# One core, a DiT layer in f32: the last four down-projection blocks multiplied by the gate ahead of their split, tile 1's residual summed in PSUM, and tile 1's other columns closed by one operation and a rank-one product

## The chip, the cores and the metric

The kernel runs on one NeuronCore of one Trainium2 chip. The metric is the device time of one execution in microseconds (us). Of the kernel before there are three timed runs, and one further execution that the hardware profiler recorded; the rows below are from that one.

The engines are named as the profile names them: PE (TensorE: matmuls, with PEld for its weight loads), DVE (VectorE), ACT (ScalarE), POOL (GpSimd) and SP (SyncE, which here only issues DMAs). PSUM is the memory in which PE leaves its products; a bank of it holds 128x512 f32.

## The reference, cut to what matters

One layer of a diffusion transformer, 256 latent tokens and 256 context tokens of width 2048, all f32. The change touches the end of it alone: the second half of the feed-forward part, its gated residual and the last layer norm.

```python
DN_ALPHA = (2.0 * DEPTH) ** 0.25        # DEPTH = 1

def layer_norm(x, g, b):
    mu = jnp.mean(x, axis=-1, keepdims=True)
    var = jnp.mean(jnp.square(x - mu), axis=-1, keepdims=True)
    return (x - mu) * lax.rsqrt(var + EPS) * g + b

def swiglu(u, w_gate, w_up, w_down):
    return (jax.nn.silu(u @ w_gate) * (u @ w_up)) @ w_down

...
x = layer_norm(DN_ALPHA * x + g1 * (heads @ w_out), ln1_g, ln1_b)
x = layer_norm(DN_ALPHA * x + g2 * swiglu(modulate(x, sh2, sc2), w_gate, w_up, w_down), ln2_g, ln2_b)
```

`w_down` is 5632 x 2048. `g2` is one vector of 2048, the same for all tokens.

## The kernel before

The 256 tokens are two tiles of 128 rows (`NT = 2`, t = 0 and 1), one token to a partition. The 2048 output columns are four chunks of `NB = 512` (n = 0 to 3). The 5632 hidden units are eleven groups f of 512, each of four pieces j of 128. `hTh[f]` and `hTl[f]` hold the hidden values transposed, as a high and a low part.

**Split products.** PE multiplies in the fast f32r form, so every f32 operand is split: ACT casts it to a high part (L230), DVE subtracts to get the low part (L231). `mm3` (L239 to L242) makes one product of three matmuls: high by high (L240), high by low weight (L241), low by high weight (L242). `load_split` loads a weight block of 512 hidden units by 512 columns (1 MB, SP queue, `raw`) and splits it in two halves of 128x1024, in tiles `hi` and `lo`; `RAW_BUFS = 4` raw tiles and `HL_BUFS = 4` of each half are there. A block gives 4 pieces x 2 tiles x 3 = 24 matmuls of 128x512.

**The end of the program.** `pair(n)` does two chunks, n and n + 1. Its list `two[0]` does chunk 2 (for some groups f by a scheme of quarters, `by_quarters`), its list `two[1]` chunk 3, in the banks "b" (tile 0) and "d" (tile 1); `whole`, returned as `two[6]`, is the order of the groups f that are not done by quarters. `plain` does one block: split, then tile 0's twelve matmuls, then tile 1's. `combine_parts`, `first_block` and `gated` multiply a finished bank by the gate (`g2[i]`, each two chunks wide) and add it to the residual base `xt`, which already holds ALPHA times the first layer norm's output.

The last four blocks of chunk 3 are handled apart: they are split into rooms that are free by then (`wide`, in the place of a tile that is no longer used, the usual `hi` and `lo`, and `hilo`, in the place of a raw tile), so that all four are there at once, and PE does tile 0 through all four and then tile 1 through all four.

**The ending.** `gated(t, 3, ...)` multiplies the bank by the gate (L1153) and adds it to `xt` (L1154), `spread` takes the statistics of chunk 3 (L1157; those of the other chunks are there already), `ln_scalars(t, True)` gets mean and 1/sqrt(var + EPS) by three Newton steps, the first on DVE (L1176, L1177), the other two on ACT (L1172 to L1174), `first_step` (L1674, four times) does (x - mean) * ln2_g, `last_step` (L1678, four times) does x * y + ln2_b, y being the root, and stores the chunk.

**What sets the order.** The program is written as one stream; a scheduler orders each engine's instructions, by its own estimate of the times, except for engines named in a `manual_schedule`, which keep the order of the text. The order is fixed in the built program. Before, the last four blocks' loads and splits are ordered by the scheduler, and only the ending itself is in the order of the text on DVE and ACT.

## Time and profile before

| | us |
|---|---|
| timed runs | 1116.37, 1119.51, 1120.67 |
| median | 1119.51 |
| profiled execution, own time | 1117.67 |
| its span, first to last instruction | 1115.9 |

How to read what follows: a row of a timeline has the start in us from the beginning of the span, the duration in us, the engine, the line of the kernel, the operation, the tiles written and read (out<-in, without buffer numbers), shapes and a count; in square brackets stands how long the engine was idle before it and who ended that wait. A row of a group has the count, the busy time in us and the mean duration of one in ns, and then the idle time before. A row of a stretch of time has the busy time of each engine with its count of instructions, then the granted clock of PE (1.00 is full), the share of the DMA engines and GB/s. Matmuls are pipelined: one lasts 0.39 us, but they start closer together.

### The profile page before, as it was taken

What the parts mean: (1) busy time and instruction counts of PE and PEld (TensorE: products, weight loads), DVE (VectorE), ACT (ScalarE), POOL (GpSimd) and SP (SyncE); (2) the same over time, 40 slices, a digit from 0 to 9 for tenths busy, and PEclk for the clock granted to TensorE, in tenths of its full rate; (3) what the DMA queues carried; (4) which work ended last, traced back from release to release, by engine and by line L of the source; (5) the groups of instructions that cost most, each with busy time, mean ns of one, the idle gap of its engine ahead of it and who ended that gap; (6) DMA issues with size and microseconds to landing.
All of it is one profiled execution on the core that took longest, in us unless ns stands there. A gap on an engine that the chain in (4) does not pass through costs nothing.

```text
span 1115.9 us, 13859 instructions
## 1 busy us (share of the span) xinstructions
PE 1095.1 (98%) x5121; PEld 886.5 (79%) x5121; DVE 895.3 (80%) x1075; ACT 602.6 (54%) x874; POOL 39.4 (4%) x86
## 2 busy tenths in 40 slices
PE   7999999999999999999999999999999999999995
PEld 6677788778878788888888888888888788888884
DVE  2469999999998898877667776887875899578886
ACT  3345675786765356445465455555644565445541
POOL 1000040102000010000000000000000000000000
PEclk9999999999999999999999999999999999999998
DMA  9999998889999789989768798899896575536651
GB/s 336 383 401 392 392 338 323 298 270 315 330 323 365 275 311 357 336 295 345 265 209 280 272 342 280 295 317 312 302 308 224 174 251 206 198 141 236 233 209 75
DMA packets 175273, 321.24 MB, mean 288 GB/s; under 512 B 8899, under 2 KB 46691, under 8 KB 172901
## 3 DMA queue, kind: packets, MB, share of 16 engines
q1 hardware_dynamic: 173718, 319.23, 81.5%
q10 hardware_dynamic: 1264, 1.11, 0.3%
q8 instruction: 40, 0.66, 0.2%
q14 instruction: 27, 0.22, 0.1%
q0 software_dynamic: 224, 0.02, 0.0%
HBM read 304.07 MB, written 16.25 MB: 287 GB/s over the span
## 4 chain that ended last, share of the span: by engine, by line
PE 93%; DVE 4%; DMA 2%; ACT 1%; issue 0%; SPq 0%; DVEq 0%; ACTq 0%
PE acc L240 22%; PE acc L242 22%; PE acc L241 22%; PE wk L242 7%; PE wk L241 7%; PE wk L240 7%; PE wk L1036 2%; PE wk L558 2%; DMA raw<-in_w_ada_dram 2%; DVE adav L359 1%; PE wk L728 1%; DMA adav<-in_b_ada_dram 1%; PE acc L1253 0%; DVE lo L237 0%; DVE m L986 0%
## 5 line engine op out<-in xcount | busy, mean ns | idle before, releaser
L231 DVE TENSOR_TENSOR lo<-raw,hi 128x1024 fp32r<-128x1024 f32 x232 | 281.1, 1222 | 126.7 <-ACT hi L230 124.8
L230 ACT CAST hi<-raw 128x1024 fp32r<-128x1024 f32 x232 | 243.8, 1055 | 242.3 <-PE acc L242 130.2
L240 PE MATMUL acc<-hi,u2h 128*128 128x512 f32 x448 | 175.4, 391 | 0.0
L242 PE MATMUL acc<-hi,u2l 128*128 128x512 f32 x448 | 174.8, 390 | 0.3 <-DVE u2l L1579 0.3
L241 PE MATMUL acc<-lo,u2h 128*128 128x512 f32 x448 | 174.7, 390 | 0.0
L359 DVE SCALAR_TENSOR_TENSOR adav<-raw,cs,adav 128x1024 f32<-128x1024 f32 (+1 forms) x96 | 114.4, 1191 | 6.3 <-DMA raw<-in_w_ada_dram 2.9
L507 ACT CAST hi<-raw 128x1024 fp32r<-128x1024 f32 x84 | 87.7, 1052 | 57.8 <-PE acc L242 36.8
L510 DVE TENSOR_TENSOR lo<-raw,hi 128x1024 fp32r<-128x1024 f32 x84 | 101.3, 1222 | 10.5 <-ACT hi L507 10.3
L240 PE MATMUL acc<-hi,hTh 128*128 128x512 f32 x264 | 102.8, 390 | 0.6 <-ACT hi L236 0.6
L240 PE MATMUL acc<-hi,uh 128*128 128x512 f32 x256 | 102.9, 402 | 0.0
L241 PE MATMUL acc<-lo,hTh 128*128 128x512 f32 x264 | 102.8, 390 | 0.0
L242 PE MATMUL acc<-hi,hTl 128*128 128x512 f32 x264 | 102.7, 390 | 0.0
L242 PE MATMUL acc<-hi,ul 128*128 128x512 f32 x256 | 100.3, 392 | 0.0
L241 PE MATMUL acc<-lo,uh 128*128 128x512 f32 x256 | 99.9, 390 | 0.0
L242 PE MATMUL wk<-hi,u2l 128*128 128x512 f32 x256 | 99.8, 390 | 0.0
L241 PE MATMUL wk<-lo,u2h 128*128 128x512 f32 x256 | 99.8, 390 | 0.0
L240 PE MATMUL wk<-hi,u2h 128*128 128x512 f32 x256 | 99.7, 390 | 0.0
L242 PEld LDWEIGHTS acc<-hi,u2l 128*128 128x128 f32 x448 | 84.2, 188 | 18.1 <-DVE u2l L1579 0.7
L240 PEld LDWEIGHTS acc<-hi,u2h 128*128 128x128 f32 x448 | 84.2, 188 | 18.1 <-ACT u2h L1578 0.8
L241 PEld LDWEIGHTS acc<-lo,u2h 128*128 128x128 f32 x448 | 84.2, 188 | 17.6 <-DVE lo L231 0.4
L240 PEld LDWEIGHTS acc<-hi,uh 128*128 128x128 f32 x256 | 48.2, 188 | 15.6 <-issue 2.1
L240 PEld LDWEIGHTS acc<-hi,hTh 128*128 128x128 f32 x264 | 49.6, 188 | 11.3 <-ACT hi L236 1.0
(296 smaller groups left out, 1730.3 us busy)
## 6 DMA issues: line engine op xcount, KB each, us to landing
raw<-in_w_ada_dram SPq DMA_DIRECT2D x64, 1024.0 KB, 8.1
raw<-in_w_gate_dram SPq DMA_DIRECT2D x44, 1024.0 KB, 6.5
raw<-in_w_up_dram SPq DMA_DIRECT2D x44, 1024.0 KB, 5.5
raw<-in_w_down_dram SPq DMA_DIRECT2D x44, 1024.0 KB, 5.2
raw<-in_w_ada_dram SPq DMA_DIRECT2D x64, 512.0 KB, 5.9
raw<-in_w_in_dram SPq DMA_DIRECT2D x18, 1024.0 KB, 7.9
raw<-in_w_out_dram SPq DMA_DIRECT2D x16, 1024.0 KB, 7.1
pd<-hx SPq DMA_DIRECT2D x64, 128.0 KB, 5.3
```

The costliest lines, as they stand in the source:

```text
L230: nc.scalar.copy(hi[:, :n], raw[:, s : s + n])
L231: nc.vector.tensor_tensor(lo[:, :n], raw[:, s : s + n], hi[:, :n].bitcast(F32), op=ALU.subtract)
L240: nc.tensor.matmul(ps, lhsT=xh, rhs=w[0], start=first, stop=False, skip_group_check=seeded)
L241: nc.tensor.matmul(ps, lhsT=xh, rhs=w[1], start=False, stop=False, skip_group_check=seeded)
L242: nc.tensor.matmul(ps, lhsT=xl, rhs=w[0], start=False, stop=last, skip_group_check=seeded)
L359: nc.vector.scalar_tensor_tensor(a[:, c : c + piece], raw[:, f : f + piece], cs[:, 4 * (g * (G4 * NB // w) + j) + 2, None], a[:, c : c + p ...
L507: nc.scalar.copy(hl.hi[:, :n], raw.t[:, s : s + n])
L510: nc.vector.tensor_tensor(hl.lo[:, :n], raw.t[:, s : s + n], hl.hi[:, :n].bitcast(F32), op=ALU.subtract)
L558: nc.tensor.matmul(bank.t[32 * j : 32 * j + 32, :width], lhsT=cs[:, 4 * k + 2 - 2 * i : 4 * k + 34 - 2 * i], rhs=raw.t[:, c * width : (c + ...
L728: nc.tensor.transpose(ps.t[:, (j * 2 + t) * P : (j * 2 + t + 1) * P], src, ident)
L1036: nc.tensor.matmul(o_ps.t[:, : 2 * P].rearrange("p (g q) -> p g q", q=32), lhsT=v, rhs=pv[:, k], start=k == 0, stop=k == 3)
```

## The change

Six things, all at the program's end:

- `two[1]` closes the banks "b" and "d" with the last ordinary block instead of with the last of the four (`pair(2, LAST)`). Both are then multiplied by the gate and added to `xt`, inside the `manual_schedule` for DVE and ACT, ahead of the last four blocks.
- Each half of the last four raw blocks is multiplied by the gate in place (L1821 of the changed kernel), then split as before. Eight multiplications of 128x1024 on DVE.
- The last four blocks go into two new banks, `ends`. That of tile 0 begins empty; into that of tile 1 ACT first copies the residual of chunk 3, so that at the end it holds the finished sum.
- Tile 0: `ends[0]` is added to `xt`, and it is closed by `ending(0)` as before.
- Tile 1, chunks 0 to 2: ahead of the end DVE puts x * ln2_g into three banks (`scaled`, L1825). When the mean is known, PE turns it into a row (L1835), ACT negates it (`less`, L1837), and PE adds -mean * ln2_g by a product with one row in the contraction (L1840). One operation, * y + ln2_b, closes each chunk (L1846).
- Tile 1, chunk 3: statistics straight from the bank (L1832), (x - mean) * ln2_g from the bank (L1845), then `last_step`. All three Newton steps are on DVE (`ln_scalars(1)` without `beside`).

```diff
@@ -58,6 +58,7 @@
 GATE_ROWS = ((17, 20, 23, 23, 24, 27), (43, 44, 47, 47, 48, 51))
 BASES = (25, 33, 45, 49)
 SEED_F = 1
+LAST = 4
 SEED_G = 2
 SLOW = 3000
 SLOW2 = 1500
@@ -1692,10 +1693,10 @@
         for n in range(4):
             last_step(t, n)
 
-    def mms(f, w, t, ps, first, last):
+    def mms(f, w, t, ps, first, last, seeded=False):
         for j in range(4):
             tt = slice(t * P, (t + 1) * P)
-            mm3(ps, hTh[f][:, j, tt], hTl[f][:, j, tt], w[j], first and j == 0, last and j == 3)
+            mm3(ps, hTh[f][:, j, tt], hTl[f][:, j, tt], w[j], first and j == 0, last and j == 3, seeded)
 
     def plain(f, n, accs, begins, ends):
         w = load_split(w_down, f * 4, n * NB)
@@ -1732,7 +1733,7 @@
         turn()
         turn()
 
-    def pair(n):
+    def pair(n, left=0):
         banks, begun, held = {}, set(), {}
 
         def bank(name):
@@ -1754,7 +1755,7 @@
             return lambda: plain(f, n, (bank("a"), bank("c")), begins("a") | begins("c"), f == whole[-1])
 
         def second(f):
-            return lambda: plain(f, n + 1, (bank("b"), bank("d")), False, f == whole[-1])
+            return lambda: plain(f, n + 1, (bank("b"), bank("d")), False, f == whole[-1 - left])
 
         def combine_parts():
             c1, u, v = (t2k(name) for name in ("c1", "u", "v"))
@@ -1794,7 +1795,7 @@
     run(one[1][1:3])
     one[3]()
     run(one[1][3:])
-    two = pair(2)
+    two = pair(2, LAST)
     run(two[0][:2])
     one[4]()
     run(two[0][2:])
@@ -1803,18 +1804,48 @@
     l2_loads()
     run(two[1][1:3])
     two[3]()
-    run(two[1][3:-4])
-    wide = pb.tile([P, 2, 2, SUB * NB], F32R, tag="u2h", name="wide")
-    wide = [[wide[:, i, j] for j in range(2)] for i in range(2)]
-    ws = [load_split(w_down, f * 4, 3 * NB, spare=i == 3, rooms=() if i else wide) for i, f in enumerate(two[6][-4:])]
-    for t in range(NT):
-        for f, w in zip(two[6][-4:], ws):
-            mms(f, w, t, two[5]("bd"[t]), False, f == two[6][-1])
+    run(two[1][3:-LAST])
+    n3 = slice(3 * NB, 4 * NB)
     with tc.manual_schedule(engines={ET.DVE, ET.Activation}):
         for t in range(NT):
             gated(t, 3, two[5]("bd"[t]), t2k("yt"))
-            spread(t, 3)
-            ending(t)
+        ends = [wk_bank() for _ in range(NT)]
+        nc.scalar.copy(ends[1], xt[:, 1, n3])
+        wide = pb.tile([P, 2, 2, SUB * NB], F32R, tag="u2h", name="wide")
+        wide = [[wide[:, i, j] for j in range(2)] for i in range(2)]
+        ws = []
+        for i, f in enumerate(two[6][-LAST:]):
+            raw = load_raw(w_down, f * 4, G4, 3 * NB, NB)
+            for s in range(0, G4 * NB, SUB * NB):
+                rv = raw[:, s : s + SUB * NB].rearrange("p (k n) -> p k n", n=NB)
+                nc.vector.tensor_mul(rv, rv, g2[1][:, None, NB:].to_broadcast([P, SUB, NB]))
+            ws.append(split_raw(raw, i == 3, () if i else wide))
+        scaled = [acc_bank() for _ in range(3)]
+        for n in range(3):
+            nc.vector.tensor_mul(scaled[n], xt[:, 1, n * NB : (n + 1) * NB], late["l2"][0][:, n * NB : (n + 1) * NB])
+        for t in range(NT):
+            for f, w in zip(two[6][-LAST:], ws):
+                mms(f, w, t, ends[t], not t and f == two[6][-LAST], f == two[6][-1], t == 1)
+        nc.vector.tensor_add(xt[:, 0, n3], xt[:, 0, n3], ends[0])
+        spread(0, 3)
+        ending(0)
+        nc.vector.bn_stats(stats[:, 1, 3, :], ends[1])
+        mu, y = norm[1] = ln_scalars(1)
+        row = wk_bank()
+        nc.tensor.matmul(row[0:1, :P], lhsT=mu, rhs=ident, start=True, stop=True)
+        less = t2k("less")[:, :P]
+        nc.scalar.activation(less[0:1, :], row[0:1, :P], AF.Copy, scale=-1.0)
+        for n in range(3):
+            sl = slice(n * NB, (n + 1) * NB)
+            nc.tensor.matmul(scaled[n], lhsT=less[0:1, :], rhs=late["l2"][0][0:1, sl], start=False, stop=True,
+                             skip_group_check=True)
+        for n in range(3):
+            sl = slice(n * NB, (n + 1) * NB)
+            if n == 1:
+                nc.vector.scalar_tensor_tensor(xt[:, 1, n3], ends[1], mu, late["l2"][0][:, n3], op0=ALU.subtract, op1=ALU.mult)
+            nc.vector.scalar_tensor_tensor(xt[:, 1, sl], scaled[n], y, late["l2"][1][:, sl], op0=ALU.mult, op1=ALU.add)
+            nc.sync.dma_start(out[0, P : 2 * P, sl], xt[:, 1, sl])
+        last_step(1, 3)
 
 
 def _rope_tables():
```

In the changed kernel every line number of the old part is one higher (L240 to L242 are L241 to L243 there). Three places in the built order:

DVE at the last four blocks, before. `lo_8963` and `lo_8967` belong to the last ordinary block; `wide`, the other `lo` and `hilo` to the last four; `acc_8411` is bank "b", `adav_6036` the gate.

```order
L231 TENSOR_TENSOR lo_8963<-raw_8960,hi_8962 128x1024
L231 TENSOR_TENSOR wide_8994<-raw_8995,wide_8994 128x1024
L231 TENSOR_TENSOR lo_8967<-raw_8960,hi_8966 128x1024
L231 TENSOR_TENSOR wide_8994<-raw_8995,wide_8994 128x1024
L231 TENSOR_TENSOR lo_9004<-raw_9001,hi_9003 128x1024
L231 TENSOR_TENSOR lo_9008<-raw_9001,hi_9007 128x1024
L231 TENSOR_TENSOR hilo_9023<-raw_9021,hilo_9023 128x1024
L231 TENSOR_TENSOR lo_9014<-raw_9011,hi_9013 128x1024
L231 TENSOR_TENSOR hilo_9026<-raw_9021,hilo_9026 128x1024
L231 TENSOR_TENSOR lo_9018<-raw_9011,hi_9017 128x1024
L1153 TENSOR_TENSOR yt_9127<-acc_8411,adav_6036 128x512
```

The same place now; `acc_8855` is bank "d", `raw_9006`, `raw_9014` and so on are the raw tiles of the last four blocks.

```order
L232 TENSOR_TENSOR lo_8963<-raw_8960,hi_8962 128x1024
L232 TENSOR_TENSOR lo_8967<-raw_8960,hi_8966 128x1024
L1154 TENSOR_TENSOR yt_8996<-acc_8411,adav_6036 128x512
L1155 TENSOR_TENSOR xt_76<-xt_76,yt_8996 128x512
L1154 TENSOR_TENSOR yt_8999<-acc_8855,adav_6036 128x512
L1155 TENSOR_TENSOR xt_76<-xt_76,yt_8999 128x512
L1821 TENSOR_TENSOR raw_9006<-raw_9006,adav_6036 128x1024 x2
L232 TENSOR_TENSOR wide_9005<-raw_9006,wide_9005 128x1024 x2
L1821 TENSOR_TENSOR raw_9014<-raw_9014,adav_6036 128x1024 x2
L232 TENSOR_TENSOR lo_9019<-raw_9014,hi_9018 128x1024
L232 TENSOR_TENSOR lo_9023<-raw_9014,hi_9022 128x1024
```

Before, all splits of the last four blocks stand ahead of the first gating; now both gatings stand ahead of the first scaling, and each block's two scalings ahead of its two splits.

PE at the end of tile 0, before: `acc_8411` is tile 0's bank, `acc_8855` tile 1's.

```order
L240 MATMUL acc_8411<-hilo_9026,hTh_7149 128x512
L241 MATMUL acc_8411<-hilo_9026,hTh_7149 128x512
L242 MATMUL acc_8411<-hilo_9026,hTl_7150 128x512
L240 MATMUL acc_8855<-wide_8994,hTh_6620 128x512
L241 MATMUL acc_8855<-wide_8994,hTh_6620 128x512
L242 MATMUL acc_8855<-wide_8994,hTl_6621 128x512
```

The same place now: `wk_9002` is `ends[0]`, `wk_9003` is `ends[1]`, `hi_9022` the second half of the second of the four blocks.

```order
L241 MATMUL wk_9002<-hilo_9045,hTh_7149 128x512
L242 MATMUL wk_9002<-hilo_9045,hTh_7149 128x512
L243 MATMUL wk_9002<-hilo_9045,hTl_7150 128x512
L241 MATMUL wk_9003<-hi_9022,hTh_6792 128x512
L242 MATMUL wk_9003<-lo_9023,hTh_6792 128x512
L243 MATMUL wk_9003<-hi_9022,hTl_6793 128x512
```

Before, all 48 matmuls of tile 1 followed tile 0's last; now 21 of them stand between those of tile 0, one or a few at a time, and 27 follow it.

DVE at the end of tile 1, before: `la` and `ly` are the Newton step, `l2_8880` is ln2_g, `l2_8881` is ln2_b.

```order
L1169 TENSOR_SCALAR ly_9167<-la_9168 128x1
L1176 TENSOR_SCALAR la_9168<-ly_9167,lv_9166 128x1
L1177 TENSOR_SCALAR ly_9167<-la_9168,ly_9167 128x1
L1674 SCALAR_TENSOR_TENSOR xt_76<-xt_76,mv_9164,l2_8880 128x512 x4
L1678 SCALAR_TENSOR_TENSOR xt_76<-xt_76,ly_9167,l2_8881 128x512 x4
```

The same place now, from the last Newton step; `acc_9048` to `acc_9050` are the three `scaled` banks.

```order
L1177 TENSOR_SCALAR la_9186<-ly_9185,lv_9184 128x1
L1178 TENSOR_SCALAR ly_9185<-la_9186,ly_9185 128x1
L1846 SCALAR_TENSOR_TENSOR xt_76<-acc_9048,ly_9185,l2_8881 128x512
L1845 SCALAR_TENSOR_TENSOR xt_76<-wk_9003,mv_9182,l2_8880 128x512
L1846 SCALAR_TENSOR_TENSOR xt_76<-acc_9049,ly_9185,l2_8881 128x512
L1846 SCALAR_TENSOR_TENSOR xt_76<-acc_9050,ly_9185,l2_8881 128x512
L1679 SCALAR_TENSOR_TENSOR xt_76<-xt_76,ly_9185,l2_8881 128x512
```

Eight operations of 128x512 behind one Newton step on DVE have become five behind three.

## The prediction

> **What bounds the kernel now.** I read the page first (busy time, chain), then the instructions in order of time where the change lies: the last 35 us. From the page, the busy line, the chain by engine, and one group, the multiplications by the gate of the last blocks:
>
> ```profile
> PE 1095.1 (98%) x5121; PEld 886.5 (79%) x5121; DVE 895.3 (80%) x1075; ACT 602.6 (54%) x874; POOL 39.4 (4%) x86
> ...
> PE 93%; DVE 4%; DMA 2%; ACT 1%; issue 0%; SPq 0%; DVEq 0%; ACTq 0%
> ...
> L1153 DVE TENSOR_TENSOR yt<-acc,adav 128x512 f32<-128x512 f32 x4 | 2.7, 685 | 9.3 <-PE acc L242 9.3
> ```
>
> PE is the bound until its last product; the DVE share of the chain is mostly what follows. DVE waits 9.3 us for PE ahead of two of those multiplications, so DVE has room here, but only late. The PE instructions at both ends of the last four blocks (first the last product of the ordinary blocks, then the first of the last four):
>
> ```profile
> 1081.30 0.39 PE L242 MATMUL acc<-hi,hTl 128*128 128x512 f32 x1
> 1081.53 0.39 PE L240 MATMUL acc<-wide,hTh 128*128 128x512 f32 x1
> ...
> 1103.06 0.39 PE L242 MATMUL acc<-hilo,hTl 128*128 128x512 f32 x1
> ```
>
> No gap between ordinary and last blocks. 96 products take 1081.53 to 1103.29, 0.227 us each, 5.44 us a block. The last ends at 1103.45. There is no gap because the split was done early: ACT cast the first half of the wide block at 1070.45 (row below), 11 us ahead. DVE behind the last product:
>
> ```profile
> 1103.49 0.69 DVE L1153 TENSOR_TENSOR yt<-acc,adav 128x512 f32<-128x512 f32 x1 [2.01 <-PE acc L242]
> 1104.21 0.69 DVE L1154 TENSOR_TENSOR xt<-xt,yt 128x512 f32<-128x512 f32 x1
> 1104.94 0.69 DVE L1157 BATCH_NORM_STATS2 stats<-xt 128x6 f32<-128x512 f32 x1
> 1105.67 0.26 DVE L1162 BATCH_NORM_AGGREGATE mv<-stats 128x2 f32<-128x24 f32 x1
> ...
> 1106.53 0.27 DVE L1176 TENSOR_SCALAR la<-ly,lv 128x1 f32<-128x1 f32 x1
> 1106.84 0.21 DVE L1177 TENSOR_SCALAR ly<-la,ly 128x1 f32<-128x1 f32 x1
> 1106.97 2.73 DVE L1674 SCALAR_TENSOR_TENSOR xt<-xt,mv,l 128x512 f32<-128x512 f32 x4
> ...
> 1109.62 2.73 DVE L1678 SCALAR_TENSOR_TENSOR xt<-xt,ly,l 128x512 f32<-128x512 f32 x4
> ```
>
> DVE works without a break from 1103.49 to 1112.35, 8.86 us; the span ends 3.55 later, with the last store. This is what the change can shorten. The own time of this execution is 1117.67 (span 1115.9 and 1.8 around it); the median of the runs, 1119.51, is 1.84 more. I work in the execution and add the difference to the median.
>
> **The change part by part.**
>
> *The gate ahead of the split.* Before, a block's split needed only its load. Now DVE stands in program order at the gating of banks "b" and "d", which need all ordinary blocks, before it scales the first raw block. Behind those waits queue every scaling and every split of the last four blocks, on ACT too, and PE waits for them. Prices of the new work, from groups and from rows in order of time:
>
> ```profile
> L1727 DVE TENSOR_TENSOR raw<-raw,sums 128x1024 f32<-128x1024 f32 x6 | 7.3, 1223 | 0.1
> L359 DVE SCALAR_TENSOR_TENSOR adav<-raw,cs,adav 128x1024 f32<-128x1024 f32 x80 | 102.4, 1280 | 4.0 <-DMA raw<-in_w_ada_dram 2.9
> L622 DVE TENSOR_SCALAR csum<-raw,cs x2: 746/750/753, 72.4 to 73.1; 128x1024 f32<-128x1024 f32 x2
> 1058.71 0.69 DVE L1766 TENSOR_TENSOR u<-wk,u 128x512 f32<-128x512 f32 x1
> 1059.31 0.69 DVE L1154 TENSOR_TENSOR xt<-xt,v 128x512 f32<-128x512 f32 x1
> 1070.45 1.05 ACT L230 CAST wide<-raw 128x1024 fp32r<-128x1024 f32 x1
> 1073.28 1.22 DVE L231 TENSOR_TENSOR lo<-raw,hi 128x1024 fp32r<-128x1024 f32 x1
> 1074.42 1.22 DVE L231 TENSOR_TENSOR wide<-raw,wide 128x1024 fp32r<-128x1024 f32 x1
> ```
>
> The scaling is a product of two tensors in place, as L1727 is: 1.22 us, and one starts 1.14 after another. Bounds: 0.75 (L622, one tensor and a scalar) and 1.28 (L359). I take 1.22, the same kind. Independent products of 512 start 0.60 apart, dependent ones 0.72 (1103.49 to 1104.21); a wake-up costs 0.04 (1103.45 to 1103.49).
>
> The gap: bank "d" is complete at 1081.69 (1081.30 and 0.39). Tile 0's gating lies under tile 1's products. Tile 1's: multiplication at 1081.73, sum 1082.45, first scaling 1083.05 to 1084.27, cast 1084.30 to 1085.35, first product 1085.4 instead of 1081.53: **3.87 late**. ACT's copy of the residual into PSUM lies beside the scaling, free. The two products of the first half can go; the third needs its low part. DVE does the second scaling first, so that low part runs 1085.40 to 1086.62: product at 1086.66, not 1085.85, **0.81 more**. From here a block costs DVE four operations, 4.6 us, PE 5.44, so PE could keep pace; but its new order asks for the next block's tile-0 products first. I walked its list against DVE's: it asks for the second block's first half at 1089.16, when the cast ends at 1089.96, **0.84**; two later waits are 0.11 and 0.16. In all PE is 5.79 late and ends at 1109.24. Loads: the raw blocks come no later than before, when the last had landed by its cast at 1079.58, ahead of all this; free.
>
> ```profile
> 1079.58 1.05 ACT L230 CAST hilo<-raw 128x1024 fp32r<-128x1024 f32 x1 [2.23 <-DMA raw<-in_w_down_dram]
> ```
>
> *The order of the tiles.* Before, 48 products of tile 1 ran behind tile 0's last, and tile 0's ending lay under them:
>
> ```profile
> 1092.61 0.69 DVE L1153 TENSOR_TENSOR yt<-acc,adav 128x512 f32<-128x512 f32 x1 [7.31 <-PE acc L242]
> 1093.34 0.69 DVE L1154 TENSOR_TENSOR xt<-xt,yt 128x512 f32<-128x512 f32 x1
> ...
> 1098.75 2.73 DVE L1678 SCALAR_TENSOR_TENSOR xt<-xt,ly,l 128x512 f32<-128x512 f32 x4
> ```
>
> From the sum (1093.34) to the end (1101.48) it takes 8.14. Now 27 products stand behind tile 0's last, 6.1 us: tile 0 is complete at 1103.1. DVE's last split ends at 1101.5, the three products with the scale row (0.60 each) at 1103.2, so neither waits long for the other. DVE is free at 1111.3, PE has been done since 1109.24: **2.05 more**, a wait that was not there.
>
> *The shorter ending of tile 1.* Gone: the multiplication, the sum, three of the first operations of L1674. Added: two Newton steps of the square root, on ACT beside DVE before, now on DVE (0.31 and 0.25 each step, as 1106.53 to 1107.09: 1.12). From the statistics on: 2.11 to the first step's end (1104.94 to 1107.05), 1.12, five operations of 0.66 (2.73 by four): 6.6 against 8.86, **2.25 saved**.
>
> Sum so far: 5.79 + 2.05 - 2.25 = 5.6 us slower.
>
> *The rank-one products.* The mean goes through PE to a row, ACT negates it, three plain f32 products of 128x512 follow. f32 shows two records a product; two such records and the next:
>
> ```profile
> 322.78 1.02 PE L377 MATMUL wk<-g1b,ones 128*128 128x512 f32 x2
> 323.23 0.80 PE L240 MATMUL acc<-hi,oTh 128*128 128x512 f32 x1
> ...
> L728 PE MATMUL wk<-ident,xt 128*128 128x128 f32 x36 | 5.4, 276 | 0.0
> L457 ACT COPY bcol<-wk 128x96 f32<-128x96 f32 x1 | 0.2, 246 | 0.0
> ```
>
> Two records last 1.02 together, one 0.59: 0.43 apart. The mean is there at 1112.3; the row takes 0.5 with its two records (0.28 one), the negation 0.25: 1113.1. Full speed: 0.86 a product, ready at 1114.3, 1115.2 and 1116.0; DVE wants them at 1114.55, 1115.9 and 1116.55: hidden, cost 0. But the clock, by stretches of time (the column before the DMA share is the granted clock):
>
> ```profile
> 1103.50:1106.50 3.00, 0.00 (x0) 0.00 (x0) 2.82 (x8) 0.00 (x0) 0.00 (x0) 1.00 0.00 0
> 1106.50:1107.50 1.00, 0.00 (x0) 0.00 (x0) 0.94 (x3) 0.38 (x2) 0.00 (x0) 0.65 0.00 0
> 1107.50:1112.00 4.50, 0.00 (x0) 0.00 (x0) 4.50 (x8) 1.20 (x5) 0.00 (x0) 0.50 0.17 65
> ```
>
> 0.65 in that stretch is 0.3 at 1.00 and 0.7 at 0.50: it fell at 1106.8, 3.35 after PE's last product. The rank-one products begin 3.9 after it, with one short product between. At half they take 1.72 each, ready at 1115.2, 1116.9 and 1118.65; DVE then ends at 1120.05, not 1117.9: **2.1 more**. Bounds 0 and 2.1; I take 2.1, since the row puts the fall before them. Total 7.7.
>
> **The rivals.**
> 1. *Rank-one products at full clock*: the short row product holds the clock. 5.6 slower: 1125.1. Against it, the row above.
> 2. *The clock falls in the gap too.* PE is empty 3.7 us (1081.69 to 1085.4), then does two products, then waits again. Half clock costs half speed in the trace: early, 12 products of one kind behind an empty stretch of 3.04 us, and 14 of them later:
>
> ```profile
> 7.97 2.93 PE L1253 MATMUL acc<-ident 128*128 128x128 f32 x12
> 16.36 1.73 PE L1253 MATMUL acc<-ident 128*128 128x128 f32 x14
> ```
>
> 0.244 us each against 0.124. Half speed from 1086.66 for some 3 us (the 2.93 above was such a stretch) loses 1.5, of which up to 0.8 hides in the wait at 1089.16: 0.7 to 1.5 on top, 1128 to 1128.7. For it, 3.7 exceeds 3.35; against, the two products. [...]
> 3. *Cheaper scaling*, 0.75 as L622: gap 0.47 shorter, the wait at 1089.16 shorter. 1.4 less: 4.2 slower, 6.3 with the slow rank-one products: 1123.7 to 1125.8.
> 4. *Not slower.* The gap at 1081.69 is the place: were the first halves scaled 5.8 us before PE wants them, PE would end on time at 1103.45, tile 0's ending run until 1105.5, and DVE end at 1112.1, 0.3 earlier than now; with DVE free at PE's end as well, 2.25 earlier: 1117.3. It decides at zero gap, and the instruction list has the gating first. So no mechanism here gives more than 0.2% of gain. That the change doesn't do what it says (a scaling that the scheduler lifted) is excluded by the same list.
>
> **How the numbers follow.** Forecast 0.42 (7.7 slower, 1127.2), rival 1 0.23, rival 2 0.18, rival 3 0.12, rival 4 0.05. Range 1121.5 to 1130.5: from rival 3 less about 2 for the spread of the runs (1116.37 to 1120.67) to rival 2 plus the same. 0.5%, about what a measurement of this kernel can tell from no change, is 5.6 us: rival 1 stands on that line. Slower: forecast 0.38, rival 2 0.17, half of rival 1 0.10: 0.65. Faster 0.03 (spread alone). Same 0.32.
>
> **What would show it.** Right: an empty PE stretch of near 3.9 us ahead of the first wide product, released by ACT, and the low part next; tile 1's statistics starting on DVE some 2 us after PE's last product; DVE's final operations released by PE at half clock. Wrong: no gap (my reading of the waits fails), scalings far from 1.22, or statistics directly behind PE.

## The result, and the profile after

| | before | after |
|---|---|---|
| median of the timed runs, us | 1119.09 (6 runs) | 1126.83 (6 runs) |
| lowest to highest | 1116.37 to 1120.67 | 1125.89 to 1128.33 |
| ratio, 95% interval | | 1.0073 [1.0058, 1.0088] |
| profiled execution, own time | 1117.67 | 1125.89 |
| its span | 1115.9 | 1124.1 |

The changed kernel is 0.7% slower. The own times differ by 8.2 us. Of the page, the busy line:

```profile
PE 1103.0 (98%) x5129; PEld 888.2 (79%) x5129; DVE 906.0 (81%) x1088; ACT 602.6 (54%) x870; POOL 39.9 (4%) x86
```

The busy line tells almost nothing: PE is 98% busy in both, though the span is 8.2 us longer; its busy time grew by 7.9, of which 5.86 are the new products at the very end (0.38 and 5.48, the last two rows of the next list) and the other 2.0 lie in the last four blocks, which PE was busy with for 23.80 us instead of 21.76. The chain that the page follows back breaks off after 2% of the span here, so its shares can't be set beside those of before. The answer is again in the last 40 us. PE, in order of time, from the last product of the ordinary blocks:

```profile
1081.38 0.39 PE L243 MATMUL acc<-hi,hTl 128*128 128x512 f32 x1
1085.49 0.73 PE L241 MATMUL wk<-wide,hTh 128*128 128x512 f32 x2 [3.72 <-ACT wide L231]
1086.75 0.79 PE L242 MATMUL wk<-wide,hTh 128*128 128x512 f32 x1 [0.53 <-DVE wide L232]
1087.35 0.63 PE L243 MATMUL wk<-wide,hTl 128*128 128x512 f32 x1
...
1109.43 0.39 PE L243 MATMUL wk<-hilo,hTl 128*128 128x512 f32 x1
1112.84 0.38 PE L1835 MATMUL wk<-ident,mv 128*1 128x128 f32 x2 [3.01 <-DVE mv L1163]
1113.57 5.48 PE L1840 MATMUL acc<-l,less 1*128 1x512 f32 x6 [0.36 <-ACT less L1837]
```

Before, the second of these rows followed the first 0.23 us later, with no wait in brackets. Now there are 3.72 us, ended by ACT's cast, and the third product waits for DVE's low part. The last row is the six records of the three rank-one products, 5.48 us. DVE in order of time, with the scalings of the four blocks and then the two endings:

```profile
1083.14 2.35 DVE L1821 TENSOR_TENSOR raw<-raw,adav 128x1024 f32<-128x1024 f32 x2
...
1087.75 2.36 DVE L1821 TENSOR_TENSOR raw<-raw,adav 128x1024 f32<-128x1024 f32 x2
...
1092.49 2.35 DVE L1821 TENSOR_TENSOR raw<-raw,adav 128x1024 f32<-128x1024 f32 x2
...
1097.24 2.36 DVE L1821 TENSOR_TENSOR raw<-raw,adav 128x1024 f32<-128x1024 f32 x2
...
1109.14 2.73 DVE L1679 SCALAR_TENSOR_TENSOR xt<-xt,ly,l 128x512 f32<-128x512 f32 x4
1111.79 0.69 DVE L1832 BATCH_NORM_STATS2 stats<-wk 128x6 f32<-128x512 f32 x1
...
1115.68 0.75 DVE L1846 SCALAR_TENSOR_TENSOR xt<-acc,ly,l 128x512 f32<-128x512 f32 x1 [0.65 <-PE acc L1840]
...
1119.09 0.75 DVE L1846 SCALAR_TENSOR_TENSOR xt<-acc,ly,l 128x512 f32<-128x512 f32 x1 [0.95 <-PE acc L1840]
1119.76 0.74 DVE L1679 SCALAR_TENSOR_TENSOR xt<-xt,ly,l 128x512 f32<-128x512 f32 x1
```

DVE has no wait from 1081.81, when bank "d" is there, until 1115.03: it goes without a wait through four blocks, tile 0's ending and tile 1's Newton steps. Its first wait behind that is for the rank-one products. Tile 1's statistics start when DVE is done with tile 0, 1.97 us after PE's last product ended (1109.82). The clock of PE, by stretches of time (the column before the DMA share):

```profile
1086.00:1086.50 0.50, 0.22 (x1) 0.00 (x0) 0.50 (x1) 0.50 (x1) 0.00 (x0) 0.79 0.00 0
...
1089.50:1090.00 0.50, 0.50 (x3) 0.46 (x2) 0.50 (x1) 0.50 (x1) 0.00 (x0) 0.80 0.00 0
1113.50:1114.00 0.50, 0.43 (x1) 0.43 (x2) 0.43 (x3) 0.02 (x1) 0.00 (x0) 0.60 0.08 25
1114.00:1119.00 5.00, 5.00 (x6) 1.37 (x5) 3.08 (x7) 0.00 (x0) 0.00 (x0) 0.50 0.13 53
```

0.79 over half a microsecond is 0.58 of it at 1.00 and 0.42 at 0.50, so the clock fell at 1086.29; in the same way it came back at 1089.70 and fell again at 1113.60, just as the rank-one products began (1113.57).

### The profile page after: what moved, and what is told of

It reads as the page before. It is cut to its first block, busy times and chain, and to the rows that moved or that the text cites. A ratio compares the mean times of both kernels' runs of the same rounds, so it can differ in the third digit from the quotient of the medians.

```text
span 1124.1 us, 13886 instructions
## 1 busy us (share of the span) xinstructions
PE 1103.0 (98%) x5129; PEld 888.2 (79%) x5129; DVE 906.0 (81%) x1088; ACT 602.6 (54%) x870; POOL 39.9 (4%) x86
## 3 DMA queue, kind: packets, MB, share of 16 engines
q10 hardware_dynamic: 1264, 1.11, 0.3%
## 5 line engine op out<-in xcount | busy, mean ns | idle before, releaser
L241 PE MATMUL acc<-hi,u2h 128*128 128x512 f32 x448 | 175.1, 391 | 0.0
L243 PE MATMUL acc<-hi,u2l 128*128 128x512 f32 x448 | 174.5, 390 | 0.4 <-DVE u2l L1580 0.4
L242 PE MATMUL acc<-lo,u2h 128*128 128x512 f32 x448 | 174.5, 389 | 0.0
L241 PE MATMUL acc<-hi,uh 128*128 128x512 f32 x256 | 102.8, 401 | 0.0
L243 PE MATMUL acc<-hi,ul 128*128 128x512 f32 x256 | 100.2, 391 | 0.0
L242 PE MATMUL acc<-lo,uh 128*128 128x512 f32 x256 | 99.8, 390 | 0.0
L243 PE MATMUL wk<-hi,u2l 128*128 128x512 f32 x256 | 99.6, 389 | 0.0
L242 PE MATMUL wk<-lo,u2h 128*128 128x512 f32 x256 | 99.6, 389 | 0.0
L241 PE MATMUL wk<-hi,u2h 128*128 128x512 f32 x256 | 99.6, 389 | 0.0
L243 PEld LDWEIGHTS acc<-hi,u2l 128*128 128x128 f32 x448 | 84.1, 188 | 18.3 <-DVE u2l L1580 0.8
L241 PEld LDWEIGHTS acc<-hi,u2h 128*128 128x128 f32 x448 | 84.1, 188 | 18.1 <-ACT u2h L1579 0.8
L242 PEld LDWEIGHTS acc<-lo,u2h 128*128 128x128 f32 x448 | 84.1, 188 | 17.7 <-DVE lo L232 0.4
L241 PE MATMUL acc<-hi,hTh 128*128 128x512 f32 x248 | 96.4, 389 | 0.6 <-ACT hi L237 0.6
L242 PE MATMUL acc<-lo,hTh 128*128 128x512 f32 x248 | 96.4, 389 | 0.0
L243 PE MATMUL acc<-hi,hTl 128*128 128x512 f32 x248 | 96.3, 389 | 0.0
L241 PEld LDWEIGHTS acc<-hi,uh 128*128 128x128 f32 x256 | 48.1, 188 | 15.6 <-ACT acc L523 2.5
L243 PEld LDWEIGHTS acc<-hi,ul 128*128 128x128 f32 x256 | 48.1, 188 | 11.0 <-DVE ul L745 0.6
```

Of the source, the lines that this page charges most:

```text
L241: nc.tensor.matmul(ps, lhsT=xh, rhs=w[0], start=first, stop=False, skip_group_check=seeded)
L242: nc.tensor.matmul(ps, lhsT=xh, rhs=w[1], start=False, stop=False, skip_group_check=seeded)
L243: nc.tensor.matmul(ps, lhsT=xl, rhs=w[0], start=False, stop=last, skip_group_check=seeded)
```

## The experiments

Upstream of the change the profiled executions differ by nearly 5 us (the last ordinary product ends at 1080.2 to 1085.1), so I compare **the stage**: from the end of the last ordinary product (its row's start and 0.39) to the span's end. Before it is 1115.9 - 1081.69 = 34.2, after 1124.1 - 1081.77 = 42.3. Line numbers differ a little from kernel to kernel. In each diff, - is the changed kernel. The stage is that of one execution each; where a kernel was run more than once, the medians, less the changed kernel's, give the same difference within 0.9 us. e2b and e8 were run once, and what is said of them is read from that one trace.

| kernel | stage, us | against after | median, us | ratio to before, 95% |
|---|---|---|---|---|
| before | 34.2 | -8.1 | 1119.09 | |
| after | 42.3 | | 1126.83 | 1.0073 [1.0058, 1.0088] |
| e1_scale_first | 36.7 | -5.6 | 1121.52 | 1.0018 [1.0002, 1.0033] |
| e5_no_scaling | 37.8 | -4.5 | 1123.23 | 1.0033 [1.0018, 1.0048] |
| e4_old_close | 41.1 | -1.2 | 1125.44 | 1.0058 [1.0042, 1.0075] |
| e3_end_held | 42.3 | 0.0 | 1127.63 | 1.0068 [1.0047, 1.0089] |
| e2b_gap_held | 42.6 | +0.3 | 1128.46, one run | |
| e3b_end_held | 40.4 | -1.9 | 1125.17 | 1.0062 [1.0049, 1.0074] |
| e6_tile0_later | 41.0 | -1.3 | 1124.93 | 1.0058 [1.0045, 1.0071] |
| e8_all_rows | 41.3 | -1.0 | 1127.54, one run | |
| e7_both_ends | 32.7 | -9.6 | 1117.53 | 0.9996 [0.9985, 1.0007] |

**Where the gating stands (e1).** The same work, but two blocks are scaled and split before DVE waits for the ordinary banks.

```diff
-        for t in range(NT):
-            gated(t, 3, two[5]("bd"[t]), t2k("yt"))
-        ends = [wk_bank() for _ in range(NT)]
-        nc.scalar.copy(ends[1], xt[:, 1, n3])
...
         for i, f in enumerate(two[6][-LAST:]):
+            if i == 2:
+                for t in range(NT):
+                    gated(t, 3, two[5]("bd"[t]), t2k("yt"))
+                ends = [wk_bank() for _ in range(NT)]
+                nc.scalar.copy(ends[1], xt[:, 1, n3])
```

> Order alone: the first two of the last four blocks are scaled and split ahead of the two gatings and of the copy of the residual into PSUM, the other two behind them; all operations stay. Theory (the empty PE stretch of 3.9 us comes from the order, since the scalings queue behind the gatings that wait for PE): the first product follows the ordinary blocks without a gap; PE then waits about 2 us each for the third and the fourth block, whose scalings come behind the gatings; PE ends some 2.6 us earlier than in the changed kernel, tile 0's ending is done before that, the rank-one products run soon enough behind PE's end to keep full clock; in all some 6.6 us less than the changed kernel, about 1120.2. Rival (the eight scalings are simply too much work for DVE there, wherever they stand): the waits only move, PE ends no earlier than now, 1126 to 1127.

The gap is gone (the first wide product starts at 1082.20, 0.22 behind the row at 1081.98), and the scheduler by itself put PE back to tile 0's products ahead of tile 1's 48. All of PE's waits that are left in the four blocks, from its instructions in order of time:

```profile
1088.34 0.51 PE L241 MATMUL wk<-hi,hTh 128*128 128x512 f32 x1 [0.53 <-ACT hi L231]
1089.60 0.50 PE L242 MATMUL wk<-lo,hTh 128*128 128x512 f32 x1 [0.76 <-DVE lo L232]
...
1092.99 0.50 PE L241 MATMUL wk<-hilo,hTh 128*128 128x512 f32 x1 [0.59 <-ACT hilo L231]
1094.25 0.50 PE L242 MATMUL wk<-hilo,hTh 128*128 128x512 f32 x1 [0.76 <-DVE hilo L232]
```

They are at the third and fourth block, since DVE does the gating between the second and the third while PE, with tile 0 first, takes a block in 2.7. PE's last product and tile 1's statistics:

```profile
1107.57 0.39 PE L243 MATMUL wk<-hilo,hTl 128*128 128x512 f32 x1
1108.00 0.70 DVE L1833 BATCH_NORM_STATS2 stats<-wk 128x6 f32<-128x512 f32 x1 [2.74 <-PE wk L243]
```

5.6 of the 8.1 us go by moving these lines, so the order on DVE is the main cause, in three ways. PE ends 25.59 after the last ordinary product (1107.96 - 1082.37), not 28.05: 2.46. The gap and what followed it are gone, but the four waits make PE 3.83 late where it was 6.29. DVE is free when PE ends: 1.93. And the ending takes 7.49 (1108.00 to 1115.49), not 8.71: 1.22, since the rank-one products run at full clock until 1111.06. I had expected 6.6, with full clock to the end; an ending of 6.72, as e3b has it further down, would have brought 0.8 of the missing 1.0. What is left against the kernel before, 2.5, is PE's 3.83 less the 1.37 by which the ending is shorter than 8.86.

**Without the scaling (e5).** The last four blocks are left without the gate, so only their split stays behind the gating.

```diff
             raw = load_raw(w_down, f * 4, G4, 3 * NB, NB)
-            for s in range(0, G4 * NB, SUB * NB):
-                rv = raw[:, s : s + SUB * NB].rearrange("p (k n) -> p k n", n=NB)
-                nc.vector.tensor_mul(rv, rv, g2[1][:, None, NB:].to_broadcast([P, SUB, NB]))
             ws.append(split_raw(raw, i == 3, () if i else wide))
```

> Leaves out the eight multiplications of the raw blocks by the gate, so chunk 3 lacks the gate on the last four blocks; the order is that of the changed kernel. Theory: the gap stays, since the gatings and the copy still stand ahead of the first cast on ACT: first product about 1085.0 instead of 1085.5, third at 1086.2 instead of 1086.75; the later waits of PE for splits go, and tile 0 is again done first, so that DVE is free when PE ends; 4.5 to 6.2 us less than the changed kernel, 1120.6 to 1122.3. Rival (the scalings' own 9 us on DVE are the gap): first product by 1082.6, and about 8 us less, 1119 or below.

ACT, and then PE, in order of time, where the first wide block begins:

```profile
1086.55 0.59 ACT L1813 COPY wk<-xt 128x512 f32<-128x512 f32 x1 [11.28 <-DVE xt L1155]
1087.08 1.99 ACT L231 CAST wide<-raw 128x1024 fp32r<-128x1024 f32 x2
1088.17 0.73 PE L241 MATMUL wk<-wide,hTh 128*128 128x512 f32 x2 [3.10 <-ACT wide L231]
```

The stage is 4.5 us shorter, but the gap only 0.6 (3.10 against 3.72), though a scaling of 1.22 is gone from it. In the changed kernel ACT's copy of the residual lay beside that scaling; here the cast queues behind the copy, which waits 11.28 us for DVE's sum. I had expected PE to gain in the four blocks, where DVE now does two operations a block instead of four. It doesn't. PE's last product, and the granted clock by stretches of time:

```profile
1112.20 0.39 PE L243 MATMUL wk<-hilo,hTl 128*128 128x512 f32 x1
```

```profile
1089.00:1089.50 0.50, 0.07 (x1) 0.07 (x1) 0.50 (x2) 0.50 (x2) 0.00 (x0) 0.83 0.00 0
...
1092.50:1093.00 0.50, 0.50 (x3) 0.38 (x2) 0.50 (x2) 0.50 (x2) 0.00 (x0) 0.75 0.00 0
```

PE ends 27.52 after the last ordinary product (1112.59 - 1085.07), only 0.53 sooner than in the changed kernel. Behind its third product, at 1089.43, it waits for nothing, and yet the 93 steps from there to the last product take 22.77, 1.7 more than 93 times 0.227: the clock is at 0.50 from 1089.33 to 1092.75, and here, where PE doesn't wait for DVE, that costs its whole price. The other 3.9 of the 4.5 lie behind PE's end. PE does tile 0 first again, so tile 1's statistics follow at once (1112.62): 1.94. And the rank-one products run at full clock until 1116.64, so the ending takes 6.73 (1112.62 to 1119.35), not 8.71: 1.98. The median, 1123.23, lies above the 1122.3 that I had as the most.

**The old closing operations (e4).** The residual stays in PSUM; the mean is taken off on DVE as before, with no rank-one product.

```diff
-        scaled = [acc_bank() for _ in range(3)]
...
-        mu, y = norm[1] = ln_scalars(1)
-        row = wk_bank()
...
+        norm[1] = ln_scalars(1, True)
         for n in range(3):
-            sl = slice(n * NB, (n + 1) * NB)
-            nc.tensor.matmul(scaled[n], lhsT=less[0:1, :], rhs=late["l2"][0][0:1, sl], start=False, stop=True,
...
+            first_step(1, n)
+        nc.vector.scalar_tensor_tensor(xt[:, 1, n3], ends[1], norm[1][0], late["l2"][0][:, n3], op0=ALU.subtract, op1=ALU.mult)
         for n in range(3):
...
+            last_step(1, n)
```

> Tile 1 closed as before: the scaled banks, the row product and the three rank-one products are gone, the mean is subtracted by four DVE operations, two Newton steps run on ACT beside them; chunk 3 still comes from its bank with the residual in it, and the gate stays ahead of the split. Theory (the rank-one products run at half clock, and DVE waits 1.9 us for them): tile 1's statistics start as now, 2 us behind PE's end, and the ending takes 7.4 us as before from there instead of 8.7: 1.3 us less than the changed kernel, 1125.5. Rival (the shorter form saves its operations): 0.8 us more, 1127.6.

DVE in order of time, from tile 1's statistics on:

```profile
1111.12 0.69 DVE L1829 BATCH_NORM_STATS2 stats<-wk 128x6 f32<-128x512 f32 x1
...
1115.80 2.73 DVE L1679 SCALAR_TENSOR_TENSOR xt<-xt,ly,l 128x512 f32<-128x512 f32 x4
```

From the statistics to the end 7.41 us (1111.12 to 1118.53), against 8.71 with the rank-one products (1111.79 to 1120.50). So of this part of the change the residual in PSUM gains (7.41 is less than the 8.86 of before), and the rank-one close loses 1.3 of it.

**The clock held at the end (e3, then e3b).** Products into a spare bank behind PE's last one, with PE's order written out as it was in the changed kernel; 24 products in e3, `range(10)` in e3b.

```diff
+        held = wk_bank()
+        for _ in range(24):
+            nc.tensor.matmul(held[:, :P], lhsT=ident, rhs=ident, start=True, stop=True)
```

> The changed kernel with PE in the same order written by hand, and 24 products of 128x128 without use behind PE's last product, 2.9 us, done before the mean is there. Theory (half clock makes the rank-one products late): granted clock 1.00 through them, 0.43 us from one record to the next instead of 0.86, no wait of DVE in the final operations, 2.0 us less than the changed kernel, 1124.8. Rival (the f32 products with one row in the contraction are slow by themselves, or the waits are the latency of the row and the negation): no change, 1126.8.

e3 is a miss of mine: each such product is two records of 0.115 us, so 24 of them last 5.52 us, and they overran the mean, which was there at 1111.24. PE in order of time:

```profile
1108.12 5.52 PE L1835 MATMUL wk<-ident 128*128 128x128 f32 x48
...
1114.30 2.84 PE L1847 MATMUL acc<-l,less 1*128 1x512 f32 x6 [0.36 <-ACT less L1844]
```

The rank-one products took 2.84 instead of 5.48 and started 2.3 late: nothing is left. With ten:

> As e3_end_held, with 10 products instead of 24: 24 took 5.5 us, two records of 0.115 us each, and kept the row product waiting 2.3 us behind the mean, which gave back what the clock had won. 10 take 2.3 us and end 0.7 us ahead of the mean. Theory (the clock alone makes the rank-one products late): the mean's row starts with the mean, records 0.43 to 0.45 us apart, no wait of DVE in the final operations, 2.0 us less from the last ordinary product to the end than the changed kernel: 40.3 instead of 42.3. Rival (the latency of row and negation): 42.3.

The same rows of e3b:

```profile
1110.16 2.39 PE L1835 MATMUL wk<-ident 128*128 128x128 f32 x20
...
1114.07 3.10 PE L1847 MATMUL acc<-l,less 1*128 1x512 f32 x6 [0.36 <-ACT less L1844]
```

Now DVE ends 6.72 after its statistics (1112.29 to 1119.01), against 8.71: the half clock at the end costs 1.99.

**The clock held in the gap (e2b).** Fourteen of the same products ahead of the 96, again with PE's order written out.

```diff
+        held = wk_bank()
+        for _ in range(14):
+            nc.tensor.matmul(held[:, :P], lhsT=ident, rhs=ident, start=True, stop=True)
```

> The changed kernel with PE in the same order written by hand, and 14 products of 128x128 without use (28 records of 0.115 us, 3.2 us) in the empty stretch of PE ahead of the first wide product. Counted from the end of the last ordinary product, 42.3 us to the span's end in the changed kernel. Theory (the clock fell in the gap, but DVE sets the pace there: its three scaled products end when tile 0's last product does): granted clock 1.00 throughout, 0.227 us a product behind the gap, PE ends 0.5 to 0.6 us earlier, the end moves by 0.2 us at most. Rival (the fallen clock is on the path): 0.6 us less, 41.7.

PE in order of time, with the waits for the second and third block:

```profile
1092.57 0.51 PE L1834 MATMUL wk<-hi,hTh 128*128 128x512 f32 x1 [0.65 <-ACT hi L231]
...
1096.69 0.61 PE L1834 MATMUL wk<-wide,hTh 128*128 128x512 f32 x2
1097.32 0.50 PE L1834 MATMUL wk<-hi,hTh 128*128 128x512 f32 x1
1097.66 0.40 PE L1834 MATMUL wk<-wide,hTl 128*128 128x512 f32 x1
...
1111.78 0.39 PE L1834 MATMUL wk<-hilo,hTl 128*128 128x512 f32 x1
```

The granted clock is 1.00 in every stretch from 1083 to 1112, and PE still ends 28.06 after the last ordinary product (1112.17 - 1084.11), as with the fall: 28.05 (1109.82 - 1081.77). I had expected 0.5 to 0.6 less. The changed kernel at the third block:

```profile
1093.88 2.14 ACT L231 CAST hi<-raw 128x1024 fp32r<-128x1024 f32 x2 [2.60 <-DVE raw L1821]
...
1095.04 0.44 PE L241 MATMUL wk<-hi,hTh 128*128 128x512 f32 x1
1095.32 0.39 PE L243 MATMUL wk<-wide,hTl 128*128 128x512 f32 x1
```

The first of two casts ends at 1094.93 (1.05 on, the time of one), and PE, slowed before by the clock, asks for it at 1095.04, just behind. At full clock PE waits 0.65 at the second block and 0.2 at the third (1097.32, where it was due two times 0.23 after 1096.69). In both the product behind the third block's first one starts 13.55 after the last ordinary product (1097.66 - 1084.11, 1095.32 - 1081.77). With the clock held the third cast, so DVE's pace, sets the end. With the fall PE, slowed, comes to the same place within 0.1 us and waits for nothing. So the half clock cost nothing here because it took the place of waits that would have been there; that the two come out equal is chance, and by my estimate, from that 0.1 us, a longer stretch at half clock would have been on the path.

**DVE late for tile 1 (e6).** Tile 0's last four operations stand behind tile 1's statistics and Newton steps.

```diff
-        ending(0)
+        norm[0] = ln_scalars(0, True)
+        for n in range(4):
+            first_step(0, n)
...
         mu, y = norm[1] = ln_scalars(1)
...
+        for n in range(4):
+            last_step(0, n)
```

> The changed kernel with tile 0's four closing operations and stores moved behind tile 1's Newton steps on DVE; no other edit. Theory (DVE is 2 us late for tile 1's statistics because tile 0's ending stands ahead of them, and that lateness also lets the clock fall ahead of the rank-one products): statistics start within 0.1 us of PE's last product; the rank-one products begin 1.9 us behind it, at full clock at least for the first two; no wait of DVE for PE, since tile 0's closing fills the time; 1.4 us less: 40.9 from the last ordinary product. Rival (the two are separate costs, and the clock falls however soon the products come): DVE waits for at least one rank-one product, and no more than 0.7 us is gained.

DVE in order of time, and the rank-one products of PE among it:

```profile
1111.40 0.70 DVE L1834 BATCH_NORM_STATS2 stats<-wk 128x6 f32<-128x512 f32 x1 [0.63 <-PE wk L243]
...
1113.19 2.91 PE L1844 MATMUL acc<-l,less 1*128 1x512 f32 x6 [0.36 <-ACT less L1841]
1114.56 2.73 DVE L1679 SCALAR_TENSOR_TENSOR xt<-xt,ly,l 128x512 f32<-128x512 f32 x4
1117.20 0.75 DVE L1850 SCALAR_TENSOR_TENSOR xt<-acc,ly,l 128x512 f32<-128x512 f32 x1
```

DVE now waits for PE ahead of the statistics, and the rank-one products lie under tile 0's four operations. 1.3 us less.

**Products over all 128 rows (e8).** The mean is spread over 128 rows, so that the closing products contract 128 rows instead of one.

```diff
-        nc.tensor.matmul(row[0:1, :P], lhsT=mu, rhs=ident, ...)
-        nc.scalar.activation(less[0:1, :], row[0:1, :P], AF.Copy, scale=-1.0)
+        nc.tensor.matmul(row[:, :P], lhsT=mu.to_broadcast([P, P]), rhs=ident, ...)
+        nc.scalar.activation(less, row[:, :P], AF.Copy, scale=-1.0 / P)
...
-            nc.tensor.matmul(scaled[n], lhsT=less[0:1, :], rhs=late["l2"][0][0:1, sl], ...)
+            nc.tensor.matmul(scaled[n], lhsT=less, rhs=late["l2"][0][:, sl], ...)
```

> The changed kernel with the three closing products made over 128 rows instead of one: the mean goes to all 128 rows of the bank, ACT multiplies it by -1/128, and each product adds 128 equal parts of -mean * ln2_g; the same output, the same columns, the same order. In the runs so far the clock fell while the one-row products ran (2.2 to 2.6 us of a 3.4 us stretch busy with them), and 5.5 us of them at half clock never raised it, though products of 128 rows raise it after 3.4 us. Theory (what the clock's control counts is the rows at work, not the time PE is busy): the clock falls as in the changed kernel if no product has begun by then, but comes back to 1.00 within 3.4 us of the first closing product, or does not fall if it is already running: six records in 4.6 us or less instead of 5.48, DVE's last wait under 0.3 us, 41.4 us or less from the last ordinary product to the end. Rival (f32 products, or short groups of them, do not raise it whatever their rows): 0.50 to the end, 5.48 us, 42.3.

The closing products on PE, and then the clock by stretches of time:

```profile
1116.51 4.18 PE L1840 MATMUL acc<-l,less 128*128 128x512 f32 x6 [0.37 <-ACT less L1837]
```

```profile
1116.00:1119.00 3.00, 2.63 (x4) 1.18 (x4) 1.91 (x8) 0.28 (x1) 0.00 (x0) 0.50 0.09 33
1119.00:1119.50 0.50, 0.50 (x2) 0.20 (x1) 0.50 (x2) 0.00 (x0) 0.00 (x0) 0.75 0.00 0
```

Here the clock comes back, at 1119.25, under the products; with one row it stayed at 0.50 through all 5.48 us. The stage is 1.0 shorter.

**Both ends mended (e7).** Tile 1's gating after two scaled blocks and tile 0's after all four, PE's order written out (each block of tile 0 as soon as it can go, with 16 of tile 1's products in between), the rank-one products issued right behind the mean, two Newton steps back on ACT, and three of tile 0's last operations ahead of tile 1's close.

```diff
-        for t in range(NT):
-            gated(t, 3, two[5]("bd"[t]), t2k("yt"))
...
+            if i == 2:
+                gated(1, 3, two[5]("d"), t2k("yt"))
+                nc.scalar.copy(ends[1], xt[:, 1, n3])
...
+        gated(0, 3, two[5]("b"), t2k("yt"))
...
+        for t, b, count in ((0, 0, 12), (0, 1, 12), (1, 0, 12), (0, 2, 12), (1, 1, 4), (0, 3, 12), (1, 1, 8), (1, 2, 12), (1, 3, 12)):
...
+        last_step(0, 0)
...
+        mu, y = norm[1] = ln_scalars(1, True, lessen)
+        for n in range(1, 4):
+            last_step(0, n)
```

> All of the found costs taken away at once: two blocks scaled and split first, then the gating of tile 1 alone and the copy, the other two blocks, the gating of tile 0; PE's order by hand (tile 0 of blocks 1 and 2, tile 1 of block 1, tile 0 of block 3, four products of tile 1, tile 0 of block 4, the rest of tile 1); three of tile 0's closing operations behind tile 1's first Newton step, the other two steps on ACT, the row ahead of them. Theory: no wait of PE over 0.3 us in the last four blocks, PE ends as early as before the change; rank-one products at full clock; from the last ordinary product to the end 33.0 us, against 34.2 before the change and 42.3 with it: 1118 to 1119, not to be told from before in time. Rival (the eight scalings cannot be placed without delay, DVE being full from there on): over 35.

PE and DVE in order of time, around tile 1's statistics:

```profile
1103.53 0.39 PE L1834 MATMUL wk<-hilo,hTl 128*128 128x512 f32 x1
1103.96 0.70 DVE L1842 BATCH_NORM_STATS2 stats<-wk 128x6 f32<-128x512 f32 x1 [0.95 <-PE wk L1834]
...
1105.74 3.78 PE L1850 MATMUL acc<-l,less 1*128 1x512 f32 x6 [0.36 <-ACT less L1847]
...
1110.61 0.74 DVE L1681 SCALAR_TENSOR_TENSOR xt<-xt,ly,l 128x512 f32<-128x512 f32 x1
```

PE has no wait in the last four blocks and ends 21.76 after the last ordinary product, as before the change. The statistics follow at once, and no operation of DVE behind them waits. The stage is 32.7, 1.5 us shorter than before's. In the timed runs that can't be told from no change: 0.9996 [0.9985, 1.0007].

## Why the prediction was right, term by term

The terms against what the trace has for them (us; after against before, in the stage). The medians moved by 7.7, with an interval of 6.5 to 9.8 (the ratio's, times 1119), so both sums agree with them.

| step of the prediction | forecast | measured |
|---|---|---|
| the gap ahead of the first wide product | 3.87 | 3.88 (1085.49, and 1081.61 without a wait) |
| the third product waits for the low part | 0.81 | 0.81 (1086.75, and 1085.94) |
| the rest of PE's lateness | 1.11 | 1.60 |
| PE late in all | 5.79 | 6.29 (28.05 against 21.76) |
| DVE late for tile 1's statistics | 2.05 | 1.93 (1.97, less 0.04 before) |
| tile 1's ending, with the rank-one products | 8.7 against 8.86 | 8.71 against 8.86 |
| sum | 7.7 | 8.1 |

**The gate ahead of the split.** The mechanism is shown by e1: with the gating behind two blocks the gap is gone. The mis-sized term is the rest of PE's lateness, by 0.5. I had it as three waits for casts (0.84, 0.11 and 0.16). None of them is in the trace: behind its third product PE has no wait left in the four blocks, since the half clock had slowed it. What e2b shows without the half clock is that the third block's cast sets PE's end, and the forecast can be compared there. By my numbers that cast ended 12.86 after the last ordinary product (1083.05, two blocks of 4.6, 1.22, 0.03 and 1.05, less 1081.69); it ends at 13.16 (1094.93 - 1081.77). Of these 0.3, half is DVE's block: 4.74 us (scalings start at 1087.75, 1092.49 and 1097.24), not the 4.6 that I took. The other half is the time from a block's first scaling to its cast, 1.39 (1092.49 to 1093.88) where I took 1.25; why it is longer stays open. The last 0.2 are PE's: its product starts 0.11 behind that cast (1095.04), and the 63 steps from there to its last product (1109.43) take 14.39, 0.1 more than 63 times 0.227. That the copy of the residual is free holds, but only beside a scaling: e5 shows it on the path (0.59 us, ahead of the first cast).

**The order of the tiles.** 1.93 for 2.05. e6 confirms it from the other side: with four of tile 0's operations moved behind tile 1's statistics, 1.3 go.

**The shorter ending, and the rank-one products.** With the clock held the ending takes 6.72 (forecast 6.6), and the half clock adds 1.99 (forecast 2.1). Rival 1, full clock, is excluded by the stretch at 0.50 (1114.00 to 1119.00). Its fall came 3.78 after PE's last product; I had counted on 3.35, as if that were fixed; it was 2.77 in e2b (1112.17 to 1114.94) and 4.11 in e4 (1109.16 to 1113.27). Here it fell 0.03 behind the start of the rank-one products, not ahead of them as I had it, and the price was paid nearly whole; that it came no later was luck.

**Rival 2 happened, and cost nothing.** I gave the fall in the gap 0.18 and 0.7 to 1.5 us. The clock did fall there, at 1086.29, so its condition was true and its price wrong: I let up to 0.8 of the loss hide, in the wait at the second block; by e2b all of it hides, there and at the third. Forecast and rival 2 had differed only by that price, so the forecast had the clock in the gap wrong and its number held by luck. Where PE doesn't wait for DVE the price is 1.7, as e5 shows. I had read that half clock is half speed from 12 early products of 0.244 us, but the granted clock is 1.00 there (8.00 to 10.00), so that row doesn't show it. The changed kernel does: at 0.50 its products start 0.43 apart (1087.35 and 1087.77), not 0.23.

**Rival 3, cheaper scaling,** falls: the scalings last 2.35 for two, as the 1.22 and the overlap of the forecast make it. **Rival 4** was rightly small for the kernel as written. e7 shows what it needed: scaling done ahead of the gap and DVE free at PE's end. I had put at most 2.25 on that; it gives 1.5.

The terms come from differences of rows, and e1 to e8 change one or two at a time. Their gains don't add up to 8.1, since in e1 and e5 PE's order on the tiles changes by itself with DVE's, and with it DVE's lateness and the clock at the end.

## What to carry to other kernels

Here an instruction that reads a late result held up what stood behind it on its engine (the scalings behind the gatings, with PE empty for 3.72 us): before moving work onto an engine's queue, look for the first wait ahead of it, and put the work that depends only on early loads in front (a few lines moved here give back 5.6 of 8.1 us). A product that replaces vector work at the very end comes to a PE that has been idle (3.01 us here); count it at half clock (six records in 5.48 us, against 3.10 behind e3b's ten products) unless something keeps the clock up or other work covers it. Price a slow clock only where PE is the bound of that stretch (nothing in the changed kernel's gap, 1.7 us in e5's).

## What the runs showed of the hardware

**In three traces the clock fell, came back 3.41 to 3.42 us later, and fell again 27.3 us after the first fall.** In the profile after, it falls at 1086.29, returns at 1089.70 (3.41 later) and falls at 1113.60 (27.31 after the first fall, 8 times 3.41). In e4 it changes at 1085.97, 1089.38 and 1113.27 (3.41 and 27.30), in e5 at 1089.33, 1092.75 and 1116.64 (3.42 and 27.31). What sets these times no run shows. The delay from PE's last product to the fall differed from kernel to kernel: 3.35 before, 3.78 after, 2.77 in e2b, 4.11 in e4. In after, e4 and e5 the fall in the first blocks came although two products (0.73 us) had run behind the gap.

**Products of one row didn't hold the clock.** In e3b PE is busy in 2.81 of the 3.5 us ahead of 1116.5 with the mean's and the rank-one products, and yet the clock falls at 1116.52:

```profile
1113.00:1116.50 3.50, 2.81 (x8) 1.12 (x8) 3.09 (x13) 0.27 (x1) 0.00 (x0) 1.00 0.30 113
1116.50:1117.00 0.50, 0.50 (x1) 0.00 (x0) 0.50 (x2) 0.00 (x0) 0.00 (x0) 0.52 0.00 0
```

In the changed kernel the clock fell 0.03 behind their start and stayed at 0.50 through the rest of their 5.48 us; in e8, with the same products over 128 rows, it was back 3.42 after the fall (1115.83 to 1119.25).
